# Two-layer encoder trunk on one Trainium2 core: block transposes share rooms, one input quarter changes from TensorE to blocks, four heads from blocks to TensorE

## Chip, cores and metric

The kernel runs on one core of one Trainium2 chip. The metric is the device time of one execution in microseconds; lower is better. All inputs are float32 in HBM, and so is the output, 256 tokens by 2048 features.

## What is computed

A trunk of two layers over 256 tokens, a grid of 4 x 64, with 2048 features. Each layer norms its input, projects it, runs 12 self-attention heads and 4 heads into 256 memory tokens, projects the 16 outputs back, adds them, and then runs a squared-ReLU MLP of width 8192.

```python
m = rms_norm(mem, mem_norm)
h = x
for i in range(2):
    n = rms_norm(h, attn_norm[i])
    if i == 0:    # neighbourhood attention with a relative-position bias
        q, k, v, qm = split(n @ a_w_in[0])
        mix = neighbourhood_attention(q, k, v, a_rpb[0])
    else:         # grouped queries: 12 query heads, 4 key heads
        q, k, v, qm = split(n @ b_w_in[0])
        q, k = axial_rope(rms_norm(q, b_q_norm[0])), axial_rope(rms_norm(k, b_k_norm[0]))
        mix = gqa_block_attention(q, k, v)
    km, vm = split(m @ w_mem_kv[i])
    cross = memory_attention(qm, km, vm)
    h = h + concat(mix, cross) @ w_o[i]
    n = rms_norm(h, mlp_norm[i])
    h = h + square(relu(n @ w_up[i])) @ w_down[i]
return rms_norm(h, final_norm)
```

## The kernel before

**Products.** Every float32 value is split into two parts, hi (a copy rounded to float32r, written by ScalarE, L441) and lo (value minus hi, written by VectorE, L442). A product is three TensorE instructions: hi with hi, hi with lo, lo with hi. Weights come from HBM in chunks of 1 MB (128 x 2048); SyncE's queue (SP) issues the loads, and each half of a chunk is split and then multiplied. Blocks of 512 output columns for two tiles of 128 tokens go through `m_products` (L314, 512-wide instructions), blocks with the tokens as the moving side through `products` (L334, 256-wide). A transpose is also a TensorE instruction (MATMUL with `ident`, 128 x 128).

**Order.** `plan` is the list of works in order. Each is cut into grains (a half chunk: 12 instructions of 512 columns). `run_all` goes through the grains: before each it traces the loads and splits of the grains ahead (3 grains for a plain work, 8/5/4 or 8/8/4 for those of the MLP), then the grain's products, then one tick. `later(n, fn)` queues a function for n ticks on. A scheduler orders each engine's instructions from this trace by priority and by its own timeline; after that the order on each engine is fixed. `past(fn, ins)` (L793) makes what fn issues come behind two given instructions, one on ScalarE and one on VectorE; `tc.issue_after(ins)` does so for the engine of one instruction; `pin` keeps program order.

**Memory.** Tiles with one tag of a pool share a number of rooms (`bufs`). A tile waits until the last user of its room is done. Pool `work` (right side) serves the attention stages; it is closed when an o projection starts and `side` is opened in its place until `to_work` (L1346) reverses that in the second layer. `ring` holds the weight chunks and their splits, `mlp` the MLP's. PSUM tags `acc` and `att` have four banks each.

**Two ways to transpose.** On TensorE: `transposed` (L453) and `attend2` (L516) put four 128 x 128 transposes per 256-wide pair into a PSUM bank, from which hi and lo are split. By blocks: VectorE transposes 32 x 32 blocks, and four transfers on SP's queue move the blocks between partition groups; `far_blocks` (L525) with `arrived` (L539) does that for a quarter (512 columns) of h, `turned` (L544) with `halved` (L559) for a head's probabilities. `far_blocks` needs a room for the blocks and a room for what lands.

**Attention.** `attention` (L578) spreads the steps of each head over ticks: scores and softmax (`attend`), the transpose, its split, and the product with the values (`attend3`). With four steps, (0, 1, 3, 4) or (0, 2, 5, 6), the transpose goes by blocks; with three, (0, 3, 6), by TensorE. In the second layer `b_qm_done` starts the four memory heads (one grain apart), and `b_q_done(blk)` starts heads 4 blk to 4 blk + 3; blocks 0 and 1 go by blocks, block 2 by TensorE. `normed_heads` (L1280) writes a block's normed and rotated heads into two tiles of tag `b_o` (three rooms), which `heads_T` transposes on TensorE.

**From the o projection to the up projection.** The o projection runs its four output blocks in two pairs (`add_o`). h is the residual; its root mean square is estimated from the first three blocks (`guard`, "near"), and the exact factor is applied later. When the third block (nb = 2) is added to h, `scaled(b)` for b = 0, 1, 2 at ticks 2, 3 and 5 scales a quarter of h (ScalarE, L819) into a tile of tag `T` and turns it by blocks into a tile of tag `b`, whose halves hold the blocks and what lands; `landed(b)` at ticks 4, 5 and 7 splits the four columns that arrived into `hT` (ScalarE L471, VectorE L472). Tags `T` and `b` have two rooms each. `begun` prepares the last quarter in a `T` tile; when the fourth block's products are done, VectorE adds them (L861), and TensorE transposes this quarter into bank `pt_n` (L459). The first up projection reads `hT` in order of k.

**From the MLP to the second layer.** The last eighth of the MLP (`plain_grains`) gives h its four blocks. `down_done(0, nb)` adds each (L1066), takes squares, and for nb < 3 turns the quarter by blocks (tick 1, two `T` tiles named `n_t`) and splits it into `nT` (tick 3); the last quarter goes through TensorE. The second layer begins with eight works for qm and k (L1352 on): quarters 0, 1 and 2 of qm, 0 of k, 3 of qm, then 1, 2 and 3 of k. The first three are loaded and split in pool `side`, the others in `ring`.

**The end.** `finish` (L1209) adds the last block of 512 columns in three pieces: all columns of tile 0, then the two 256-column halves of tile 1. For each, ScalarE squares and sums, VectorE adds the mean square to the running one, and behind a tile's last piece GpSimd takes the power -1/2, VectorE and ScalarE scale, and the rows are stored.

Of the kernel before, what the change touches and what calls it, by code (L numbers as in the profile page):

```python
# [70 lines left out]
class Work:  # L71


    def __init__(self, kind, src, acts, first, begins, last, start, done):
        self.kind, self.src, self.acts = kind, src, acts
        self.first, self.begins, self.last, self.start, self.done = first, begins, last, start, done
        self.early = self.behind = self.last_block = False
# [48 lines left out]
def encoder_kernel(ctx: ExitStack, tc: tile.TileContext, t: dict, out: bass.AP):  # L126
# [82 lines left out]
    box: dict = {}  # L209
# [5 lines left out]
    def halves_of(w):  # L215
# [9 lines left out]
        def prep(hf):  # L225
            if hf == 0:
                n = plan.index(w)
                if n in soon:
                    tiles["raw"] = soon.pop(n)
                else:  # L230
                    tiles["raw"] = at.ring.tile([P, CH], F32, tag="raw", bufs=3, name="raw")
                    nc.sync.dma_start(tiles["raw"], w.src)
            src = tiles["raw"][:, hf * HALF : (hf + 1) * HALF]
            if w.behind and hf == 1:

                tiles[hf] = new_half(w.kind)
                past(lambda: split(*tiles[hf], src), box["cat" if w.last_block else "pT", NH - 2])
            elif plan[plan.index(w) - 1].last_block:

                tiles[hf] = new_half(w.kind)  # L240
                past(lambda: split(*tiles[hf], src), box["cat", NH - 1])
            elif w.kind == "S" and hf == 0 and plan[plan.index(w) - 1].kind == "M":
                tiles[hf] = entered_half(src)
            else:
                tiles[hf] = new_half(w.kind)
                split(*tiles[hf], src)
# [269 lines left out]
    def attend2(sc):  # L516
        pt = at.att.tile([P, NT, SEQ], F32, tag="att", name="pt_a")
        for s in range(NT):
            i = NT - 1 - s
            for k in range(NT):  # L520
                nc.tensor.transpose(pt[:, k, i * P : (i + 1) * P], sc[:, s, k * P : (k + 1) * P], ident)
        pT = at.work.tile([P, 2, NT, SEQ], F32R, tag="pT", name="pT")
        return pT, split(pT[:, 0], pT[:, 1], pt)
# [15 lines left out]
    def arrived(dst, raw, k0, which):  # L539

        for n in range(4):
            split_pair(dst, raw[:, :, :, n], which, k0 + n, by_quarters=True)

    def turned(sc):  # L544
# [7 lines left out]
        pT = at.work.tile([P, 2, 4, NT, NT * 32], F32R, tag="pT", name="pT_t")  # L552
# [246 lines left out]
    def o_done(layer, nb):  # L799
# [16 lines left out]
        def scaled(b):  # L816
            y = at.side.tile([P, NT, 512], F32, tag="T", bufs=2, name="h_s")
            for i in range(NT):
                nc.scalar.activation(y[:, i, :], h[:, i, b * 512 : (b + 1) * 512], AF.Copy,  # L819
                                     scale=box["scale"][:, i : i + 1])  # L820
            room = at.side.tile([P, 2, 1024], F32, tag="b", bufs=2, name="h_t")
            box["raw", b] = far_blocks(lambda i: y[:, i, :], (room[:, 0], room[:, 1]))
# [13 lines left out]
        def f(w):  # L836
# [67 lines left out]
    def up_grains(layer, part, m):  # L904
# [24 lines left out]
        def run(hf):  # L929
# [14 lines left out]
            products(own["ps"], box["hT" if part else "hT0"], hf * (KT // 2), KT // 2, *own.pop(hf), keep_order=part > 0,  # L944
                     first=own.pop("first", None))
# [234 lines left out]
    def down_done(layer, nb):  # L1180
        def f(w):
# [27 lines left out]
    def finish(w, i, bank, begin, end):  # L1209
# [10 lines left out]
        q = small.tile([P, 1], F32, tag="ss0", name="ss_f")  # L1220
        sq = at.side.tile([P, 512], BF16, tag="junk", bufs=1, name="sq")
        nc.scalar.activation(sq[:, begin:end], hs, AF.Square, accum_out=q)
# [7 lines left out]
        m = box["mean"] = mean(q, box["mean"])  # L1230
# [49 lines left out]
    def normed_heads(w):  # L1280
        cg, sg = box["rope"]
        outs = []
        for i in range(NT):
# [10 lines left out]
            o = at.work.tile([P, 4, HD], F32, tag="b_o", bufs=3, name="b_o")  # L1294
# [22 lines left out]
    def b_q_done(blk):  # L1317
        def f(w):
# [5 lines left out]
                       for j, kv in enumerate(kvs)], 1, 2, (0, 3, 6) if blk == 2 else (0, 2, 5, 6),  # L1324
# [3 lines left out]
    def b_qm_done(w):  # L1328
# [3 lines left out]
        for i in range(NT):  # L1332
# [8 lines left out]
                   for j in range(NMH)], 1, 1)  # L1341
# [4 lines left out]
    def to_work():  # L1346
        closed("side")
        open_work()
        mem_back()
# [6 lines left out]
    plan[-6].early = "last"  # L1356
    add_m(blocks(4), parts_of("nT"), b_v_done)
# [13 lines left out]
    later(26, x_stats)  # L1371
# [132 lines left out]
```

## Time and profile before

| | us |
|---|---|
| median of three runs | 2013.01 |
| lowest, highest | 2012.42, 2015.40 |
| the profiled execution, its own time | 2015.48 |
| span of its instructions | 2013.7 |
| mean granted TensorE clock over the span | 0.998 |
| VectorE, ScalarE busy | 1703.7, 1270.0 |

A row of a timeline shows start, duration, engine, line, operation, output<-inputs, shape and count; in brackets the engine's idle time before it and what ended that. A row of a stretch shows its length and the busy time of TensorE, of its weight loads, of VectorE, ScalarE and GpSimd with instruction counts, then the granted clock, the share of the DMA engines and GB/s. TensorE's instructions overlap: one lasts longer than the distance to the next, so the rate is read from start to start (0.227 us for 512 columns, 0.113 to 0.12 for 256). A TensorE wait is idle time only where nothing else was in flight.

### The profile page before, as it was taken

To read this page: it belongs to the slowest core of one execution; us is meant where nothing else is said; L and a number is where in the kernel's file an instruction comes from. 1 tells how busy PE (TensorE), PEld (TensorE's weight loads), DVE (VectorE), ACT (ScalarE), POOL (GpSimd) and SP (SyncE) were. 2 spreads that over 40 slices of the span, in tenths; PEclk is the share of its full clock that TensorE was granted. 3 is DMA by queue.
4 is the path that set the end of the run, shared out by engine and by line. 5 is a ranking of instruction groups with operands and counts; after the bars stand their busy time and mean duration, and the time that the engine had idled before them with its cause. 6 is when DMAs were issued, how large, how long until landed. Compare 5 with 4: busy or idle time off the path is not lost.

```text
span 2013.7 us, 32879 instructions
## 1 busy us (share of the span) xinstructions
PE 1999.8 (99%) x12948; PEld 1815.4 (90%) x12948; DVE 1703.7 (85%) x2110; ACT 1270.0 (63%) x1732; POOL 117.7 (6%) x144
## 2 busy tenths in 40 slices
PE   9999999999999999999999999999999999999998
PEld 8999999899999999999988888789999999999997
DVE  6777777579999999999997769778999999999896
ACT  6655555466676666666655557566766666666664
POOL 0000000000000000000000001000000000000000
PEclk9999999999999999999999999999999999999999
DMA  8766655757777777777767455547777777777763
GB/s 294 303 196 209 211 193 195 262 164 248 229 230 234 231 222 235 232 233 234 229 205 261 157 206 181 208 147 236 234 231 232 232 234 235 228 239 223 236 215 131
DMA packets 103083, 445.93 MB, mean 221 GB/s; under 512 B 10896, under 2 KB 36496, under 8 KB 55440
## 3 DMA queue, kind: packets, MB, share of 16 engines
q1 hardware_dynamic: 85824, 411.84, 58.4%
q0 software_dynamic: 16816, 31.46, 9.0%
q8 instruction: 101, 1.65, 0.3%
q10 hardware_dynamic: 288, 0.52, 0.1%
q14 instruction: 54, 0.44, 0.1%
HBM read 398.17 MB, written 4.19 MB: 200 GB/s over the span
## 4 chain that ended last, share of the span: by engine, by line
PE 92%; DVE 3%; DMA 1%; ACT 1%; SPq 1%; issue 1%; DVEq 0%; POOL 0%; POOLq 0%; ACTq 0%
PE ps_u L346 34%; PE ps_s L346 10%; PE p L1025 9%; PE p L1026 9%; PE p L1023 9%; PE ps_m L326 7%; PE ps_m L323 7%; PE ps_m L327 7%; DMA pT_t<-sc_t 1%; DMA h_t<-h_t 1%; SPq L555 1%; DVE lo L442 1%; SPq L535 0%; ACT hi L441 0%; DVE h_t L532 0%
## 5 line engine op out<-in xcount | busy, mean ns | idle before, releaser
L346 PE MATMUL ps_u<-hT,uh 128*128 128x256 f32 x3780 | 659.1, 277 | 1.0 <-ACT hT L471 0.8
L346 PEld LDWEIGHTS ps_u<-hT,uh 128*128 128x128 f32 x3780 | 574.6, 188 | 6.7 <-ACT hT L471 1.1
L346 PE MATMUL ps_u<-hT,ul 128*128 128x256 f32 x1940 | 536.4, 277 | 0.0
L441 ACT ACTIVATE uh<-raw_U 128x1024 fp32r<-128x1024 f32 x266 | 282.1, 1061 | 248.7 <-PE ps_u L346 227.7
L346 PEld LDWEIGHTS ps_u<-hT,ul 128*128 128x128 f32 x1940 | 364.4, 188 | 0.0
L442 DVE TENSOR_TENSOR lo<-raw,hi 128x1024 fp32r<-128x1024 f32 (+1 forms) x215 | 255.0, 1190 | 114.3 <-ACT hi L441 113.7
L442 DVE TENSOR_TENSOR ul<-raw_U,uh 128x1024 fp32r<-128x1024 f32 x266 | 322.9, 1218 | 25.5 <-ACT uh L441 25.3
L441 ACT ACTIVATE hi<-raw 128x1024 fp32r<-128x1024 f32 (+1 forms) x215 | 222.7, 1039 | 176.1 <-PE ps_m L327 92.0
L441 ACT ACTIVATE bh<-b 128x2048 fp32r<-128x2048 f32 x112 | 215.3, 1922 | 98.3 <-PE p L1026 92.2
L442 DVE TENSOR_TENSOR bl<-b,bh 128x2048 fp32r<-128x2048 f32 x112 | 256.1, 2287 | 11.4 <-ACT bh L441 11.4
L442 DVE TENSOR_TENSOR tl<-t,th 128x1536 fp32r<-128x1536 f32 x112 | 196.5, 1754 | 42.2 <-ACT th L441 41.0
L441 ACT ACTIVATE th<-t 128x1536 fp32r<-128x1536 f32 x112 | 166.8, 1489 | 40.7 <-PE p L1026 38.7
L1026 PE MATMUL p<-bh,a_s 128*128 128x512 f32 x448 | 175.1, 391 | 0.0
L1025 PE MATMUL p<-bl,a_s 128*128 128x512 f32 x448 | 174.5, 390 | 0.2
L1023 PE MATMUL p<-bh,a_s 128*128 128x512 f32 x448 | 174.3, 389 | 0.0
L995 POOL DMA_DIRECT2D b<-b x112 | 97.0, 866 | 1133.2 <-DVE t L994 983.5
L346 PE MATMUL ps_s<-nT,hi 128*128 128x256 f32 x896 | 155.0, 276 | 0.0
L346 PEld LDWEIGHTS ps_s<-nT,hi 128*128 128x128 f32 x896 | 135.6, 188 | 0.2
L1023 PE MATMUL p<-th,a_s 128*128 128x512 f32 x336 | 131.4, 391 | 0.0
L1025 PE MATMUL p<-tl,a_s 128*128 128x512 f32 x336 | 131.2, 390 | 0.0
L1026 PE MATMUL p<-th,a_s 128*128 128x512 f32 x336 | 130.7, 389 | 0.0
L346 PE MATMUL ps_s<-nT,lo 128*128 128x256 f32 x448 | 124.0, 277 | 0.0
(273 smaller groups left out, 3581.9 us busy)
## 6 DMA issues: line engine op xcount, KB each, us to landing
raw_U<-in_w_up SPq DMA_DIRECT2D x128, 1024.0 KB, 4.9
b<-in_w_pair SPq DMA_DIRECT2D x112, 1024.0 KB, 4.9
raw<-in_w_o SPq DMA_DIRECT2D x32, 1024.0 KB, 4.9
b<-b POOLq DMA_DIRECT2D x112, 256.0 KB, 3.4
raw<-in_w_b SPq DMA_DIRECT2D x21, 1024.0 KB, 4.9
raw<-in_w_av SPq DMA_DIRECT2D x12, 1024.0 KB, 4.9
raw<-in_w_aq SPq DMA_DIRECT2D x12, 1024.0 KB, 5.1
raw<-in_w_ak SPq DMA_DIRECT2D x12, 1024.0 KB, 4.8
```

Source lines behind the costliest of these rows:

```text
L323: first = nc.tensor.matmul(ps, ah, hi[:, s], start=st, stop=False)
L326: nc.tensor.matmul(ps, ah, lo[:, s], start=False, stop=False)
L327: final = nc.tensor.matmul(ps, al, hi[:, s], start=False, stop=sp)
L346: ins = nc.tensor.matmul(ps, x, acts[:, k, part], start=k == n == 0, stop=k == KT - 1 and n == 2)
L441: first = nc.scalar.activation(dst_hi, src, AF.Copy)
L442: return first, nc.vector.tensor_tensor(dst_lo, src, dst_hi.bitcast(F32), op=ALU.subtract)
L555: nc.sync.dma_start(raw[:, a].rearrange("p k c -> p (k c)"), blocks[a * 32 : (a + 1) * 32].rearrange("p b k t j -> p (b k t j)"))
L995: nc.gpsimd.dma_start(b[:, 3, :], b[:, 1, :], accum_op=ALU.add)
L1023: ins = nc.tensor.matmul(ps, a[:, 0, ai, :], hi[:, s], start=begins, stop=False)
L1025: nc.tensor.matmul(ps, a[:, 0, ai, :], lo[:, s], start=False, stop=False)
L1026: nc.tensor.matmul(ps, a[:, 1, ai, :], hi[:, s], start=False, stop=ends)
```

## The change

The block transposes of the o projection's output share rooms: for b = 0 and 1 the scaled quarter lies in one half of the `b` tile, its blocks in the other, and what lands goes over the scaled quarter; b = 2 takes a `T` tile for these two and the blocks half of the first `b` tile. `scaled(2)` moves from tick 5 to 4, all of them come behind the newest weight split, and the first up product is held behind the last o product. The last quarter of the second layer's input is turned by blocks too, later ticks apply to quarters 2 and 3, and one weight split (of quarter 1 of k) comes behind the arrival. Block 1's heads (4 to 7) use the three-step way; `pT` has three rooms in the second layer, `b_o` two; the memory heads there start two grains apart. The mean squares at the start run one tick sooner, from other rooms. The last piece's mean square is one VectorE instruction.

```diff
+            elif w.waits and hf == 0:
+                tiles[hf] = new_half(w.kind)
+                past(lambda: split(*tiles[hf], src), box["arrived"])
...
-                split(*tiles[hf], src)
+                box["weights"] = split(*tiles[hf], src)
...
-        pT = at.work.tile([P, 2, NT, SEQ], F32R, tag="pT", name="pT")
+        pT = at.work.tile([P, 2, NT, SEQ], F32R, tag="pT", bufs=2 + box["layer"], name="pT")
...
-            split_pair(dst, raw[:, :, :, n], which, k0 + n, by_quarters=True)
+            box["arrived"] = split_pair(dst, raw[:, :, :, n], which, k0 + n, by_quarters=True)
...
-                sq = at.work.tile([P, 512], F32, tag="b_y2", name="sq")
+                sq = at.work.tile([P, 512], F32, tag="b_y", name="sq")
...
         def scaled(b):
-            y = at.side.tile([P, NT, 512], F32, tag="T", bufs=2, name="h_s")
+            if b < 2:
+                box["room", b] = at.side.tile([P, 2, 1024], F32, tag="b", bufs=2, name="h_t")
+                y = box["room", b][:, 0]
+            else:
+                y = at.side.tile([P, 1024], F32, tag="T", bufs=2, name="h_s")
...
-            room = at.side.tile([P, 2, 1024], F32, tag="b", bufs=2, name="h_t")
-            box["raw", b] = far_blocks(lambda i: y[:, i, :], (room[:, 0], room[:, 1]))
+            box["raw", b] = far_blocks(lambda i: y[:, i * 512 : (i + 1) * 512], (box["room", b % 2][:, 1], y))
...
-                for b in range(GUARD):
-                    later((2, 3, 5)[b], scaled, b)
-                    later((4, 5, 7)[b], landed, b)
-                later(7, begun)
+                for n, fn, *args in ((2, scaled, 0), (3, scaled, 1), (4, scaled, 2), (4, landed, 0), (5, landed, 1),
+                                     (7, landed, 2), (7, begun)):
+                    later(n, lambda fn=fn, args=args: past(lambda: fn(*args), box["weights"]))
...
+            with tc.issue_after(box["late"].ins) if part == m == hf == 0 else nullcontext():
+                products(own["ps"], box["hT" if part else "hT0"], hf * (KT // 2), KT // 2, *own.pop(hf),
+                         keep_order=part > 0, first=own.pop("first", None))
...
-            if nb < 3:
-                def turn():
-                    room = [at.side.tile([P, 1024], F32, tag="T", bufs=2, name="n_t") for _ in range(2)]
-                    box["raw"] = far_blocks(lambda i: h[:, i, nb * 512 : (nb + 1) * 512], room)
-                later(1, turn)
-                later(3, lambda: arrived(box["nT"], box["raw"], nb * 4, G_A1))
-            else:
-                later(1, transposed, box["nT"], lambda i, k: h[:, i, k * P : (k + 1) * P], list(range(12, KT)), G_A1)
+            def turn():
+                room = [at.side.tile([P, 1024], F32, tag="T", bufs=2, name="n_t") for _ in range(2)]
+                box["raw"] = far_blocks(lambda i: h[:, i, nb * 512 : (nb + 1) * 512], room)
+            def come():
+                arrived(box["nT"], box["raw"], nb * 4, G_A1)
+            for n, fn in (((1, turn), (3, come)), ((3, turn), (5, come)), ((1, turn), (4, come)))[max(nb - 1, 0)]:
+                later(n, lambda fn=fn: past(fn, box["splits"][-1]) if nb == 2 or nb == 3 and fn is turn else fn())
+            if nb == 3:
...
+        if begin:
+            m = small.tile([P, 1], F32, tag="rs_v", name="fin_v")
+            sq = at.side.tile([P, 3, 512], F32, tag="T", bufs=2, name="sq_t")[:, 0, : end - begin]
+            nc.vector.tensor_tensor_reduce(sq, hs, hs, 1.0 / D, box["mean"], ALU.mult, ALU.add, m)
+        else:
+            q = small.tile([P, 1], F32, tag="ss0", name="ss_f")
+            sq = at.side.tile([P, 512], BF16, tag="junk", bufs=1, name="sq")
+            nc.scalar.activation(sq[:, begin:end], hs, AF.Square, accum_out=q)
...
-            o = at.work.tile([P, 4, HD], F32, tag="b_o", bufs=3, name="b_o")
+            o = at.work.tile([P, 4, HD], F32, tag="b_o", bufs=2, name="b_o")
...
-                       for j, kv in enumerate(kvs)], 1, 2, (0, 3, 6) if blk == 2 else (0, 2, 5, 6),
+                       for j, kv in enumerate(kvs)], 1, 2, (0, 3, 6) if blk else (0, 2, 5, 6),
...
-                   for j in range(NMH)], 1, 1)
+                   for j in range(NMH)], 1, 2)
...
+        box["layer"] = 1
...
+    plan[-3].waits = True
...
-        later(3 + j, mem_squares, j)
+        later(min(3 + j, 9), mem_squares, j)
-    later(11, mem_stats)
+    later(10, mem_stats)
...
-    later(26, x_stats)
+    later(25, x_stats)
```

More of the change, by code (lines that the diff above doesn't have):

```diff
@@ L1 @@
 import math
-from contextlib import ExitStack
+from contextlib import ExitStack, nullcontext
 import numpy as np
@@ L76, in __init__ @@
         self.first, self.begins, self.last, self.start, self.done = first, begins, last, start, done
-        self.early = self.behind = self.last_block = False
+        self.early = self.behind = self.last_block = self.waits = False
 class Shifted:
@@ L206, in gain @@
         return gains[:, which * KT + k : which * KT + k + 1]
-    box: dict = {}
+    box: dict = {"layer": 0}
     plan: list = []
@@ L551, in turned @@
                                 sc[:, s, :].rearrange("p (k i b) -> p k b i", k=NT, b=4))
-        pT = at.work.tile([P, 2, 4, NT, NT * 32], F32R, tag="pT", name="pT_t")
+        pT = at.work.tile([P, 2, 4, NT, NT * 32], F32R, tag="pT", bufs=2 + box["layer"], name="pT_t")
         raw = pT[:, 1].bitcast(F32)
@@ L1229, in finish @@
             box["mean"] = v
-        m = box["mean"] = mean(q, box["mean"])
+            m = box["mean"] = mean(q, box["mean"])
         if end < 512:
```

7 lines of the change are left out of this document (1 added, 6 removed).

## The prediction

> **What bounds the kernel now.** I read the page first (its busy line), then the table of waits of TensorE, then TensorE's timeline around every wait in it, and last the other engines' timelines there.
>
> ```profile
> PE 1999.8 (99%) x12948; PEld 1815.4 (90%) x12948; DVE 1703.7 (85%) x2110; ACT 1270.0 (63%) x1732; POOL 117.7 (6%) x144
> ```
>
> TensorE (PE) sets the time: it is idle for 13.9 us of the 2013.7, and some 8 of those lie behind its last product. So a change can only give back what PE loses in stalls, add or remove PE instructions, or shorten the tail. The stalls:
>
> ```profile
> PE ps_m L323 <- ACT cat L441: 1.8, 2, 1.4
> PE av L570 <- DVE pT_t L442: 1.0, 1, 1.0
> ...
> PE ps_u L346 <- ACT hT L471: 0.8, 1, 0.8
> PE ps_m L326 <- DVE ul L442: 0.5, 1, 0.5
> PE pt_n L459 <- DVE h_s L861: 0.5, 2, 0.3
> ```
>
> Columns: total us, times, longest. They stand in four places: the second layer's last heads (cat, pT_t), the entry into each layer's up projection (hT, h_s), and the entry into the second layer (ul). A stall costs more than its idle time, as the granted clock shows:
>
> ```profile
> 1268.00:1272.00 4.00, 2.63 (x18) 2.24 (x17) 3.73 (x7) 3.93 (x11) 0.00 (x0) 1.00 0.42 172
> 1344.00:1348.00 4.00, 3.72 (x20) 3.52 (x19) 4.00 (x7) 3.75 (x6) 0.00 (x0) 0.63 0.00 0
> 1348.00:1352.00 4.00, 4.00 (x35) 4.00 (x34) 3.83 (x7) 2.13 (x6) 0.00 (x0) 0.94 0.76 266
> ```
>
> The column behind POOL is the clock: 0.63 and 0.94 behind the stall at 1342, that is 4 x 0.37 + 4 x 0.06 = 1.7 us of full speed lost, but 1.00 around the equally long stall at 1269.
>
> **The up projection's input, second layer.** The same instructions run at this place in both layers, so the layers can be laid side by side:
>
> ```profile
> 426.26 0.38 PE L459 MATMUL pt_n<-ident,h_s 128*128 128x128 f32 x2
> ...
> 427.54 0.40 PE L346 MATMUL ps_u<-hT,uh 128*128 128x256 f32 x2
> 428.11 0.87 PE L459 MATMUL pt_n<-ident,h_s 128*128 128x128 f32 x6 [0.17 <-DVE h_s L861]
> ...
> 431.44 0.28 PE L346 MATMUL ps_u<-hT,uh 128*128 128x256 f32 x1
> ...
> 1341.24 0.38 PE L459 MATMUL pt_n<-ident,h_s 128*128 128x128 f32 x2
> ...
> 1342.05 0.28 PE L346 MATMUL ps_u<-hT,ul 128*128 128x256 f32 x1
> 1343.18 0.91 PE L346 MATMUL ps_u<-hT,uh 128*128 128x256 f32 x2 [0.85 <-ACT hT L471]
> ...
> 1349.76 0.28 PE L346 MATMUL ps_u<-hT,uh 128*128 128x256 f32 x1
> ```
>
> From the pair of transposes to the last row layer 1 takes 431.44 - 426.26 = 5.18 us, layer 2 1349.76 - 1341.24 = 8.52: 3.34 us lost, the 1.7 of the clock among them. What is late is the third quarter of hT:
>
> ```profile
> 419.94 1.07 DVE L532 STREAM_TRANSPOSE h_t<-h_s 128x512 f32<-128x512 f32 x1
> 425.96 1.71 ACT L471 ACTIVATE hT<-h_t,first 128x256 fp32r<-128x256 f32 x4 [2.69 <-DMA h_t<-h_t]
> ...
> 1329.98 1.71 ACT L471 ACTIVATE hT<-h_t,first 128x256 fp32r<-128x256 f32 x4 [1.00 <-DMA h_t<-h_t]
> 1335.18 1.07 DVE L532 STREAM_TRANSPOSE h_t<-h_s 128x512 f32<-128x512 f32 x1
> 1342.62 1.71 ACT L471 ACTIVATE hT<-h_t,first 128x256 fp32r<-128x256 f32 x4 [4.10 <-DMA h_t<-h_t]
> ```
>
> Its blocks go into a room that the first quarter leaves only when its splits are done, behind 1329.98 + 1.71; the second transpose ends at 1336.25, and the split starts 6.4 us later (5.0 in layer 1). With shared rooms the blocks need only the first quarter's landing, 1329.98. Behind one weight split of 1.2 us and the two transposes of 1.07 they end near 1333, and the split starts 5.0 to 6.4 later, at 1338 to 1339.5. PE asks at 1342.2: 3 us of margin. So I take the whole **3.34** (1.6 without the clock's 1.7, should another wait bring it down there, to 3.34). The Trainium skill, "TensorE: Matmul & The Clock Gate", Part 1, lets the clock fall after a window of about 3.4 us without work; here it fell behind idle pieces of 0.85, 0.13 and 0.28 us, so the trace does not agree, and by the rule, with the drop owed to something else, the sum would come out 1.7 us higher.
>
> The 0.17 us wait of pt_n on h_s, in both layers, is VectorE finishing the third quarter before L861; starts 427.54 to 428.11 against 0.23 for two products make 0.34 us a layer; I take half of the two, **0.35** (0 to 0.7).
>
> The waits added here: scaled and landed come behind the newest weight split on ACT and DVE. That split is due in the same grain, and what queues behind it (squares of the mean, weight splits three grains ahead) has those grains' 2.7 us each as cover; price 0. The up weights' split into room "b" now waits for the third landing as well, about 1338, while PE first reads it at 1347: also 0. Holding the first up product behind the last o product only keeps the order that PE shows.
>
> **Heads 4 to 7 on TensorE.** In order: TensorE, then two ScalarE rows.
>
> ```profile
> 1259.13 1.04 PE L1276 MATMUL pt_h<-ident,b_o 128*128 128x128 f32 x8
> 1261.19 0.39 PE L570 MATMUL av<-pT_t,vb 128*128 128x256 f32 x1 [1.02 <-DVE pT_t L442]
> ...
> 1269.43 0.28 PE L497 MATMUL sc_ps<-kT,qT 128*128 128x256 f32 x1
> 1271.08 0.50 PE L323 MATMUL ps_m<-hi,cat 128*128 128x512 f32 x1 [1.37 <-ACT cat L441]
> 1271.42 0.40 PE L326 MATMUL ps_m<-lo,cat 128*128 128x512 f32 x1
> ...
> 1290.10 0.39 PE L570 MATMUL av<-pT,vb 128*128 128x256 f32 x1 [0.17 <-DVE pT L442]
> 1291.43 0.50 PE L323 MATMUL ps_m<-hi,cat 128*128 128x512 f32 x1 [0.47 <-ACT cat L441]
> ...
> 1253.01 0.48 ACT L508 ACTIVATE sc<-sc_ps,nm 128x256 f32<-128x256 f32 x1 [0.58 <-DVE sc_t L550]
> 1266.83 0.63 ACT L441 ACTIVATE pT_t<-pT_t 128x512 fp32r<-128x512 f32 x1 [2.86 <-DMA pT_t<-sc_t]
> ```
>
> Four stalls: idle 1.02 + 1.37 + 0.17 + 0.47 = 3.03 us. Each also costs 0.16 (a 256-wide product lasts 0.28 in a slot of 0.12) and 0.11 at the restart (1271.08 to 1271.42 is 0.34 against 0.23): 4 x 0.27 = 1.08, so 4.1 in all. Heads 6 and 7 are late because their probabilities go through blocks, four transfers and a split that waits for them, and because the blocks take one of three "sc" rooms, for which the exponential at 1253.01 waits. The new path has neither. I let the first two stalls go (2.93) and half of the last two (0.6), which are heads 8 to 11, already on this path: **-3.5** (0 to -4.1).
>
> The price is 16 transposes on PE. Eight took (1.04 - 0.27) / 7 = 0.11 us a start at 1259.13; the upper bound is this group:
>
> ```profile
> L521 PE MATMUL pt_a<-ident,sc 128*128 128x128 f32 x16 | 2.7, 272 | 0.0
> ```
>
> 2.7 / 16 = 0.17. So 1.8 to 2.7; I take **+2.1**, nearer the start-to-start figure, since a transpose between products overlaps them. VectorE loses eight block transposes (0.6 us each), SP 16 transfers; the split costs the same. The freed SP queue lets w_o loads go sooner; no wait of PE in the table is for one of them.
>
> A third pT room costs nothing; a third b_o room goes, which would matter if a block's heads were written before the last block's were transposed: those transposes are over at 1226, the next block writes from 1238, 12 us of cover. Memory heads two grains apart end at most three grains (8 us) later than 1164, and their first reader runs at 1226.
>
> **Input of the second layer, last quarter.** TensorE, ScalarE, SyncE:
>
> ```profile
> 1092.03 0.73 PE L323 MATMUL ps_m<-uh,nT 128*128 128x512 f32 x2
> 1093.30 0.50 PE L326 MATMUL ps_m<-ul,nT 128*128 128x512 f32 x1 [0.53 <-DVE ul L442]
> ...
> 1086.67 1.71 ACT L471 ACTIVATE nT<-n_t,first 128x256 fp32r<-128x256 f32 x4 [5.09 <-DMA n_t<-n_t]
> ...
> 1081.56 2.59 SPq L535 DMA_DIRECT2D n_t<-n_t  x4
> ...
> 1084.85 22.36 SPq L232 DMA_DIRECT2D raw<-in_w_b  x6
> ```
>
> ScalarE stood 5.09 us before the third quarter's split, so the weight split behind it came late and PE lost 1.27 - 0.45 = 0.82, with the restart 0.9. Moving that quarter two grains on, behind the weight split, takes the wait out of the way. Eight PE transposes go: 8 x 0.11 = 0.9. Together -1.8. Against that stand four more transfers on SP among the loads at 1084.85, and four products of VectorE and ScalarE each. The last quarter is first read by the fourth work of the q block, the fifth of the stage in program order: 24 products of 0.23 us a work from 1083.5 on make 1083.5 + 4 x 5.44 = 1105.3. VectorE can turn it from about 1094, when the third quarter's landing frees the rooms; with the 5.1 us from issue to split seen here it is split by about 1102. I take **-1.7** (from -1.8 to the second rival's loss).
>
> **Tail and start.**
>
> ```profile
> 2006.57 0.42 ACT L1222 ACTIVATE sq<-first 128x256 bf16<-128x256 f32 x1 [1.66 <-DVE first L1218]
> ...
> 2005.02 0.42 DVE L1232 TENSOR_TENSOR first<-first,gf 128x256 f32<-128x256 f32 x1
> ...
> 2007.11 0.16 DVE L1213 SCALAR_TENSOR_TENSOR fin_v<-ss_f,fin_v 128x1 f32<-128x1 f32 x1 [0.63 <-ACT sq L1222]
> ```
>
> From 2006.57 to 2007.27 the last mean square takes 0.70 on two engines; one VectorE instruction over 256 columns that also reads its sum takes between 0.42 (L1232) and 0.42 + 0.19 (ScalarE's sum read): **-0.2** (-0.3 to 0). The earlier mean squares at the start move no PE instruction out of a stall: 0 (+-0.2).
>
> **Sum**, against the profiled execution's 2015.48: -3.34 - 0.35 - 3.5 + 2.1 - 1.7 - 0.2 = -7.0, so 2008.5. The median of the runs shown, 2013.01, lies 2.5 below that execution; if its runs lack the 1.7 us at the low clock, the gain is 5.3 there, and 2013.01 - 5.3 = 2007.7. Between the two: **2008.0**.
>
> **Rivals.**
> - *Everything goes.* Last stalls of the heads and of h_s go too: another -0.95 and the low price of the transposes, -0.3: 2006.5 to 2007. For it: VectorE gets lighter at all four places.
> - *The second layer's last quarter is late (slower).* SP issues in order; if its four transfers stand behind the six loads, they are issued at 1107.2, landed and split by 1107.2 + 2.6 + 2.9 + 2 = 1114.7, and PE stands from 1105.3 for up to 9.4 us, and the low clock adds 1.7; the split that the change puts behind the arrival holds ScalarE and VectorE meanwhile. Time 2008.0 + 1.7 + 11.1 = 2020.8; it passes 2017.0 (0.2% slower) when the splits are done later than about 1111. Against it: of the stage's eight works six don't need that quarter, so PE can have work until 1116.
> - *The heads' stall moves.* ScalarE and VectorE feed heads 8 to 11 at the same pace, so half of the 4.1 us stays and the transposes are paid: +0.05 in place of -1.4: 2009.5 to 2010.5. For it: the two stalls at 1290 are on the new path already.
> - *Transposes let the clock fall.* If they did not count as work, eight of them with the 1.02 us idle behind would have cost the clock; one drop costs 1.7: 2009.7. The clock was 1.00 there (1268 to 1272 too). The Trainium skill, the same page, Part 4, says that transposes do not count as busy in the same way for the gate, and by that rule the 16 added would bring drops; the trace does not bear it out at 1259, where no drop follows.
>
> **Chances.** Forecast 0.50 (2006.8 to 2009.6), everything 0.18, moved stall 0.17, late quarter 0.09, clock 0.06. About 0.2% (4.0 us) is what a measurement of this kernel can tell from no change; that is 2009.0. Faster: 0.38 of the forecast's 0.50 and the 0.18, with 0.02 of the others: 0.58. Same: 0.12 + 0.15 + 0.05 + 0.03 = 0.35. Slower: 0.07 of the late quarter. Range 2005.5 to 2012.5, which leaves out most of the late quarter and the ends of the others.
>
> **What would show it.** Right: no wait of ps_u on hT near 1342 and a clock of 1.00 there; no waits on cat or pT_t near 1260 to 1271; 16 more pt_a and 8 fewer pt_n; no wait of ps_m on nT before 1110; the first power of the tail's last piece 0.2 us sooner behind the last product. Wrong: a wait on ACT nT in the second layer's entry, new waits on pT near 1250 to 1290, or products that start slower than 0.113 and 0.227 us apart with the rooms moved.

## The result, and the profile after

The changed kernel takes 2014.18 us (median of 14 runs, 2011.92 to 2015.31) beside 2013.16 for the kernel before on the same chip (14 runs): ratio 1.0002, 95% interval 0.9994 to 1.0011. No difference can be told. The forecast was 2008.0. The profiled execution of after took 2014.38 us, with a span of 2012.6.

Table of waits of TensorE, after (total us, times, longest); the first group that is new stands on top:

```profile
PE ps_m L327 <- ACT hi L445: 3.1, 1, 3.1
PE ps_m L327 <- ACT uh L445: 0.7, 1, 0.7
PE pt_n L463 <- DVE h_s L869: 0.6, 2, 0.3
```

The waits on cat, pT_t, hT and ul that the prediction quoted are gone; two waits for weight splits have come, at the entry into the second layer. TensorE's timeline there, after:

```profile
1093.83 0.39 PE L331 MATMUL ps_m<-uh,nT 128*128 128x512 f32 x1
1097.30 1.22 PE L327 MATMUL ps_m<-hi,nT 128*128 128x512 f32 x2 [3.09 <-ACT hi L445]
1099.20 1.22 PE L327 MATMUL ps_m<-uh,nT 128*128 128x512 f32 x2 [0.67 <-ACT uh L445]
1100.22 0.63 PE L330 MATMUL ps_m<-lo,nT 128*128 128x512 f32 x1
1100.64 0.63 PE L331 MATMUL ps_m<-hi,nT 128*128 128x512 f32 x1
```

and the stretches around it (granted clock in the column behind POOL):

```profile
1096.00:1100.00 4.00, 2.02 (x4) 1.21 (x5) 2.72 (x3) 3.81 (x4) 0.00 (x0) 0.59 1.06 407
1100.00:1104.00 4.00, 4.00 (x11) 3.10 (x11) 4.00 (x4) 2.05 (x3) 0.00 (x0) 0.55 1.11 311
1344.00:1348.00 4.00, 3.71 (x33) 3.52 (x32) 4.00 (x5) 2.15 (x4) 0.00 (x0) 1.00 0.00 0
```

TensorE stands 3.1 us, then 0.7, and then works at half clock: 1100.22 to 1100.64 is 0.42 us where 0.227 is the full rate. The clock is low from 1096.74 to 1103.57. At 1344, where it fell before, it is now 1.00.

To compare stages I use one measure below, TensorE's **loss**: over all neighbouring products of a stretch, the distance from start to start less 0.2266 us (512 columns), 0.1135 (256) or 0.11 (transposes), added up. Idle time, restarts and a low clock are all in it.

| loss, us | 0:160 | 1080:1120 | 1240:1320 | 1320:1400 |
|---|---|---|---|---|
| before | 5.4 | 0.9 | 4.9 | 5.3 |
| after | 5.4 | 6.9 | 1.0 | 1.0 |

The two later places gave back 8.2 us, more than forecast. The entry into the second layer took 6.0 of it, the 8 transposes more (16 added, 8 removed) 0.9; what is left, 1.4 (1.3 by these rounded losses), is by how much sooner the last product starts (2004.27 against 2005.67).

This profiled execution of before is a costly one at 1342. Of its 5.3 there, 1.7 are the low clock, and 1.4 come from 1348 to 1388, where the 256-wide products start 3.6% slower than 0.1135 us apart at a clock of 1.00. A second profile of the same kernel (experiment 11, called before again) has neither, and loses 2.2 there. The same stretch in before and in before again:

```profile
1368.00:1380.00 12.00, 12.00 (x104) 12.00 (x103) 9.21 (x14) 6.41 (x9) 0.94 (x1) 1.00 0.69 220
1368.00:1380.00 12.00, 12.00 (x109) 12.00 (x108) 8.65 (x11) 7.46 (x10) 1.02 (x2) 1.00 0.67 212
```

Against before again the change gives back 5.2 us at the two later places and 0.7 at the start, and loses 6.1 at the entry and 0.9 for transposes; its last product starts 0.9 later (2004.27 against 2003.38), which is near what the medians show.

**What is late at 1094.** ScalarE's timeline, then SyncE's queue, then GpSimd, all after:

```profile
1088.81 1.06 ACT L445 ACTIVATE uh<-raw_U 128x1024 fp32r<-128x1024 f32 x1 [1.15 <-PE ps_m L331]
1092.21 1.72 ACT L475 ACTIVATE nT<-n_t,first 128x256 fp32r<-128x256 f32 x4 [2.34 <-DMA n_t<-n_t]
1096.19 2.00 ACT L445 ACTIVATE hi<-raw 128x1024 fp32r<-128x1024 f32 x2 [2.26 <-DMA raw<-in_w_b]
1098.10 1.99 ACT L445 ACTIVATE uh<-raw_U 128x1024 fp32r<-128x1024 f32 x2
...
1083.04 1.93 SPq L539 DMA_DIRECT2D n_t<-n_t  x3
1085.01 0.60 SPq L909 DMA_DIRECT2D raw_U<-in_w_b  x1
1085.66 0.61 SPq L539 DMA_DIRECT2D n_t<-n_t  x1
1086.31 2.21 SPq L232 DMA_DIRECT2D raw<-in_w_b  x3
...
1088.15 0.71 POOL L1218 TENSOR_TENSOR rstd<-full,mhalf 128x2 f32<-128x2 f32 x1 [69.23 <-DVE full L794]
1088.82 0.60 POOL L677 DMA_DIRECT2D km<-mem_k  x1
```

ScalarE, then GpSimd, before:

```profile
1090.94 1.04 ACT L441 ACTIVATE uh<-raw_U 128x1024 fp32r<-128x1024 f32 x1
1092.26 2.01 ACT L441 ACTIVATE hi<-raw 128x1024 fp32r<-128x1024 f32 x2 [0.28 <-DMA raw<-in_w_b]
1094.18 1.04 ACT L441 ACTIVATE uh<-raw_U 128x1024 fp32r<-128x1024 f32 x1
...
1091.51 0.71 POOL L1205 TENSOR_TENSOR rstd<-full,mhalf 128x2 f32<-128x2 f32 x1 [72.71 <-DMA raw<-in_w_b]
1092.34 0.60 POOL L673 DMA_DIRECT2D km<-mem_k  x1
```

Call the stage's works 1, 2, 3 and so on. A work is 24 products, two halves of 12, and each split named uh is one half. From 1085.89 to 1094.05 TensorE runs 36 products of uh with nT: work 1 and the first half of work 2 (split at 1088.81). What it lacks then is weights: the second half of work 2 is the first of the two splits from 1098.10. On ScalarE this split stands behind that of the first ring chunk (the two splits of raw from 1096.19). The order was the same before (1090.94, 1092.26, 1094.18), but there the chunk had landed at 1092.24. The third quarter of nT is not what TensorE waits for: it is split from 1092.2 to 1095.9, and its first reader, work 3, starts only near 1109.

Three things changed together. TensorE comes sooner: without the wait and the transposes that stood there it is through the first half of work 2 at 1094.05, before at 1095.7. The chunk is issued 1.5 us later (1086.31 against 1084.85), since the transfers of the third quarter stand ahead of it on SyncE's queue and begin 1.5 us later (1083.04 against 1081.56). And it takes 9.9 us (1086.31 to 1096.17) where before it took 7.4. The longer transfer has a neighbour that was not there before: the reload of the memory keys and values, which GpSimd issues behind the power of rstd. The mean square for rstd no longer queues behind the third quarter's split, so the power comes 3.4 us sooner and the reload 3.5. Which of these costs what had to be tried.

### The profile page after: what moved, and what is told of

Read it like the earlier page. It is cut to its first block, busy times and chain, and to the rows that moved or that the text cites. A ratio compares the mean times of both kernels' runs of the same rounds, so it can differ in the third digit from the quotient of the medians.

```text
span 2012.6 us, 32835 instructions
## 1 busy us (share of the span) xinstructions
PE 1997.9 (99%) x12956; PEld 1812.4 (90%) x12956; DVE 1703.2 (85%) x2105; ACT 1270.2 (63%) x1730; POOL 117.8 (6%) x144
## 4 chain that ended last, share of the span: by engine, by line
PE 93%; DMA 2%; DVE 2%; ACT 1%; issue 1%; SPq 0%; POOL 0%; POOLq 0%; DVEq 0%; ACTq 0%
PE ps_u L350 33%; PE p L1035 9%; PE p L1036 9%; PE p L1033 9%; PE ps_s L350 8%; PE ps_m L330 7%; PE ps_m L331 7%; PE ps_m L327 7%; DMA raw<-in_w_b 0%; ACT hi L445 0%; DMA raw_l<-in_w_km 0%; PE sc_ps L500 0%; PE av L573 0%; PE av L574 0%; PE sc_ps L499 0%
```

## The experiments

**1. Third quarter back on its old ticks**, the last one still by blocks.

```diff
-for n, fn in (((1, turn), (3, come)), ((3, turn), (5, come)), ((1, turn), (4, come)))[max(nb - 1, 0)]:
-    later(n, lambda fn=fn: past(fn, box["splits"][-1]) if nb == 2 or nb == 3 and fn is turn else fn())
+for n, fn in ((1, turn), (4, come)) if nb == 3 else ((1, turn), (3, come)):
+    later(n, lambda fn=fn: past(fn, box["splits"][-1]) if nb == 3 and fn is turn else fn())
```

> The changed kernel, but the third quarter of the second layer's input keeps its old ticks (turned one grain on, split three grains on, not behind a weight split); the last quarter still goes by blocks. Measure: how much TensorE loses between 1080 and 1120 us against one product every 0.227 us (0.9 us before the change, 6.9 after). Theory A, the third quarter was moved too far: with it split some 6 us sooner PE has the third work of the q block to do again while the first ring chunk comes; loss 1 to 2 us, time about 2014.2 - 5 = 2009. Theory B, the first ring chunk is late because other transfers run beside it: it still lands after 1094, loss 3 to 5 us, time 2010.5 to 2012.5. Theory C, the last quarter's own blocks are to blame: loss stays near 6.9, time 2014.

Measured 2011.21 us, before 2013.22; ratio 0.9988 (0.9979 to 0.9997). Loss 1080:1120 is 4.2. The reload moves with the third quarter (issued at 1091.8 again) and the chunk lands at 1091.6. The 4.2 lies in theory B's range, but the chunk is not late any more, so no theory had it in this shape. ScalarE, then TensorE:

```profile
1104.67 1.71 ACT L475 ACTIVATE nT<-n_t,first 128x256 fp32r<-128x256 f32 x4 [7.21 <-DMA n_t<-n_t]
...
1091.63 0.73 PE L327 MATMUL ps_m<-uh,nT 128*128 128x512 f32 x2 [0.97 <-ACT uh L445]
1092.89 0.50 PE L330 MATMUL ps_m<-ul,nT 128*128 128x512 f32 x1 [0.53 <-DVE ul L446]
...
1107.38 0.73 PE L327 MATMUL ps_m<-hi,nT 128*128 128x512 f32 x2 [0.53 <-ACT hi L445]
1108.64 0.50 PE L330 MATMUL ps_m<-lo,nT 128*128 128x512 f32 x1 [0.53 <-DVE lo L446]
```

Some 2.6 us go between 1088 and 1100, where the transposes of the last quarter had stood, and 1.6 at 1104 to 1109, where ScalarE stands 7.2 us for the last quarter and the weight split ordered behind it is late. So the move of the third quarter (theory A) cost a part, the fall from 6.9 to 4.2, but not in A's way: here too work 3 comes behind the chunk, and what came sooner is the chunk. Another part, 1.6, is the weight split ordered behind the last quarter, which is nearest to theory C, though the loss did not stay near 6.9.

**2. Reload held back**: one GpSimd instruction that reads two columns of the second ring chunk stands in front of it (`mem_back` is traced two ticks later, so that this chunk is known).

```diff
+g = nc.gpsimd.tensor_tensor(gate[:, :NT], box["ring2"][:, :NT], mhalf[:, :NT], op=ALU.mult)
+with tc.issue_after(g.ins):
     nc.gpsimd.dma_start(box["km"], mem_k)
...
```

> The changed kernel, but the reload of the memory keys and values on GpSimd's queue (issued from 1088.8 in the changed kernel, from 1092.3 before) waits until the second ring chunk has landed: one GpSimd instruction that reads two columns of that chunk stands in front of it. The order of all other engines is the same. Theory A (third quarter too late): the third quarter is split as late as before, near 1095.9, but the ring chunk decides what PE starts with; if the chunk lands where it did (1096.2) the loss stays 6 to 7 us, time 2014. Theory B (the reload shares the DMA engines with the ring chunk): the chunk lands about 1.9 us sooner, near 1094.3; the wait of 3.1 us falls to about 1.2, and with it perhaps the stretch at half clock (3.4 us more): loss 1.5 to 5 us, time 2009 to 2012.3. Theory C (last quarter): no change, 2014.

2011.47 us; ratio 0.9991 (0.9982 to 1.0). Loss 4.5. ScalarE and TensorE:

```profile
1093.83 2.01 ACT L447 ACTIVATE hi<-raw 128x1024 fp32r<-128x1024 f32 x2 [0.73 <-DMA raw<-in_w_b]
...
1094.94 0.73 PE L329 MATMUL ps_m<-hi,nT 128*128 128x512 f32 x2 [1.26 <-ACT hi L447]
1096.83 1.22 PE L329 MATMUL ps_m<-uh,nT 128*128 128x512 f32 x2 [1.16 <-ACT uh L447]
```

The chunk now takes 8.3 us (issued at 1085.56) against 9.9, so the reload beside it cost 1.6; in experiment 4, where the reload went out only at 1106, the chunk took 7.9. The wait falls from 3.1 to 1.3 and the half clock from 6.8 us to 3.4. Theory B holds, for 2.4 of the 6.0 (these 2.4 and the parts found with experiments 1 and 8 overlap and do not add up).

**3. The whole second layer's input as before**, all else changed (the loop of `down_done` as in the old code, and no `waits`).

> The changed kernel with the whole second layer's input as it was: third quarter on its old ticks, last quarter through TensorE (8 transposes more), no weight split behind the arrival. All other parts of the change stay. If this part alone ate the gain (A, B or C): loss between 1080 and 1120 back to about 0.9, time 2014.2 - 6.0 + 0.9 for the transposes = 2009 (2008 to 2009.5). If the loss there comes from elsewhere (the other parts push the stage): loss 4 to 7, time 2013 to 2015.

2008.41 us (2007.72 to 2010.41); ratio 0.9977 (0.9968 to 0.9986). Loss 0.8. This part of the change ate the gain of the others. TensorE here:

```profile
1089.95 0.38 PE L463 MATMUL pt_n<-ident,first 128*128 128x128 f32 x2
...
1090.63 0.82 PE L463 MATMUL pt_n<-ident,first 128*128 128x128 f32 x6
1091.21 0.72 PE L327 MATMUL ps_m<-uh,nT 128*128 128x512 f32 x2
1092.46 0.50 PE L330 MATMUL ps_m<-ul,nT 128*128 128x512 f32 x1 [0.53 <-DVE ul L446]
```

The eight transposes run while TensorE would have to wait for the weight split at 1091 anyway. In experiment 1, with the third quarter on the same ticks but without these transposes, the same place has waits of 0.97 and 0.53: removing the transposes saved nothing.

**4. Only the new input, on the kernel before.**

> The kernel before with only the new treatment of the second layer's input (later ticks for the third quarter, last quarter by blocks, one weight split behind the arrival). A, B or C: it loses the 6 us alone and saves the 8 transposes' 0.9: 2013.2 + 5.0 = 2018 (2017 to 2019.5). If the loss needs the other parts too: 2012.5 to 2014.

2014.86 us; ratio 1.0008 (0.9999 to 1.0016): less harm than expected, and by the time alone not told from none. Loss 1080:1120 is 2.75, with waits of 1.0 and 1.2 at the same two splits as in experiment 2, but the clock stayed at 1.00 and the reload, held by another room, went out only at 1106. So the loss at the entry does not need the other parts, but with them it is larger. This execution also lost some 1.6 us between 428 and 472, where the products ran 3.6% slow (see the end). And the loss at 1342 had vanished (loss 1320:1400 of 0.6), although that code was the old one. That put the largest term of the prediction in doubt.

**5, 6, 7. One of the other parts alone, on the kernel before**: the rooms; the heads; the mean squares at start and end. Each edit is the lines of the diff that belong to it.

> The kernel before with only the shared rooms of the block transposes between the o and the up projection (with the new ticks and the order behind the weight splits). Theory P (the prediction): the second layer's entry lost 3.34 us in every execution and the rooms give it back: 2013.2 - 3.3 - 0.35 = 2009.5 (2009 to 2010.5). Theory J: the loss at 1342 was an event of the one profiled execution, in which one of four transfers landed 4.2 us after its issue instead of 2.7; a typical execution has at most the idle waits of pt_n there, so the rooms move the median by 0 to -0.8: 2012.4 to 2013.2.

> The kernel before with only the heads' part of the change (heads 4 to 7 on TensorE, three rooms for pT, two for b_o, memory heads two grains apart). The prediction's sum: -3.5 + 2.1 = -1.4, 2011.8. With the price that the other runs' counts suggest (16 x 0.11 = 1.76) and all four stalls gone (TensorE's loss between 1240 and 1320 us from 4.9 to about 1.0): -3.9 + 1.8 = -2.1, 2011.1. Rival (the stall moves to heads 8 to 11): loss 2.5 to 3 stays there, 2012.6 to 2013.2. Beside it, the second layer's entry of the kernel before is seen once more: Theory P says a loss near 3.3 us between 1320 and 1360, Theory J about 0.5.

> The kernel before with only the mean squares: at the start one tick sooner and from other rooms, at the end one VectorE instruction for the last piece. The prediction's sum: 0 and -0.2, 2013.0. The rival from the other traces: TensorE's loss in the first 160 us falls from 5.4 to 4.4 with the start's part, so -1.0 - 0.3 = 2011.9. And the second layer's entry of the kernel before once more: P a loss near 3.3 between 1320 and 1360, J about 0.5.

| | us | ratio, interval | 0:160 | 1240:1320 | 1320:1400 |
|---|---|---|---|---|---|
| rooms | 2011.79 | 0.9990 (0.9981, 0.9999) | 5.6 | 5.0 | 0.9 |
| heads | 2010.17 | 0.9983 (0.9974, 0.9992) | 6.0 | 0.9 | 0.9 |
| mean squares | 2011.71 | 0.9991 (0.9982, 1.0000) | 4.6 | 4.9 | 3.8 |

(before 2013.59 us, 33 runs.) The rooms bring 1.8 by the medians, between theories P and J. The heads bring 3.4, more than the 2.3 of their own stage (loss -4.1, 16 transposes at 0.11 +1.8), since the loss at 1342 is gone there too. The mean squares bring 1.9, where the prediction had 0.2. Each interval is some 1.8 us wide to either side, so only the heads' gain is well clear of none. The three sum to 7.1, and all together (experiment 3) bring 4.8; the loss at 1342, which the rooms and the heads each remove, counts twice in the 7.1. The loss at 1342 is seen in the run with the mean squares and not in the one with the heads, with the same code: something else decides. (The 3.8 has no drop of the clock in it, but the same slow stretch as before's profile, 1.6 us from 1344 to 1388.)

**8. Experiment 1 without the order behind the arrival.**

```diff
-    plan[-3].waits = True
```

> The changed kernel with the third quarter on its old ticks (as in the earlier run that had only this) and without the order that puts the first weight split of quarter 1 of k behind the arrival of the last quarter. In that earlier run TensorE lost 4.2 us between 1080 and 1120: 2.6 at 1088 to 1100 where the eight transposes had stood, 1.6 at 1104 to 1109 behind that weight split. If the order behind the arrival costs the second part, it goes: loss 2.6, time 2011.2 - 1.6 = 2009.6. If the last quarter itself is late by then, PE waits for nT instead and the loss stays 3.5 to 4.5: 2011. The first part should stay, since nothing covers the wait for the weight split any more.

2008.82 us (2008.15 to 2009.47); ratio 0.9973 (0.9964 to 0.9982). Loss 2.5: the 1.6 at 1104 to 1109 is gone, nT of the last quarter is not late, and the waits of 1.0 and 0.5 stay where the transposes had been. So the last quarter by blocks can be had, and gains nothing: 0.9 for the transposes, and 1.7 more of loss than in experiment 3; beside before, both are 4.8 us faster.

The 6.0 come apart in three steps: from after to experiment 1 the third quarter's later ticks, 6.9 to 4.2; from there to experiment 8 the split ordered behind the arrival, 4.2 to 2.5; from there to experiment 3 the wait that the transposes had covered, 2.5 to 0.8.

**9, 10, 11. What makes hT late at 1342?** The DMA queues between 1340.0 and 1341.2, before (packets, MB, share of the 16 engines):

```profile
q1 hardware_dynamic: 223, 0.11, 40.7%
q8 instruction: 1, 0.02, 4.9%
```

One packet of 16 KB that loads instructions takes 0.95 us (4.9% of 16 engines over 1.2 us, one engine's time) while the four transfers of h_t run. The last of the four landed 4.2 us after its issue; the three others and all eight of the quarters ahead took 2.7 to 3.1. There are 101 such loads to 12,948 products, one for 128 on average, so a change in the number of TensorE's instructions moves all those behind it. Three runs: before with 2 instead of 10 idle products at the start; the heads' part with 2; before again.

```diff
-    for _ in range(10):
+    for _ in range(2):
         nc.tensor.matmul(idle, ones, ones, start=True, stop=True)
```

> The kernel before with 2 instead of 10 idle products of TensorE at its very start, nothing else: 8 float32 products fewer, so every load of 16 KB of instructions falls later in TensorE's stream (all those behind the start). Theory F: the third quarter's last transfer landed late at 1342 because one load of instructions (at 1340.2, 0.95 us on one DMA engine, 3.9 us behind the first of the four issues) ran among them; in the runs where the count of TensorE's instructions before this place was 16 lower or 32 higher it fell elsewhere and no wait on hT was left. Then here it falls 1.4 to 1.8 us later, behind the transfers: the four transfers land 2.7 to 3.0 us after their issues, no wait on hT, loss between 1320 and 1400 about 0.6 to 0.9 in place of 5.3. Rival, the loss belongs to the rooms and the late issue alone: wait on hT of 0.8 to 1.0 stays, loss 3.8 to 5.3. The start can lose up to 1.5 us, since the clock rises later; median 2012 to 2013.5 by F, 2013.5 to 2015 by the rival.

> The run with only the heads' part (16 transposes more), again with 2 instead of 10 idle products at the start: the 16 transposes moved the load of instructions to 1.7 us behind the first of the four issues, and the fewer idle products bring it back by about as much, to 3 to 3.9 us behind it. Theory F: the wait on hT comes back, the last transfer lands 3.9 to 4.5 us after its issue, loss between 1320 and 1400 from 0.9 to 3.5 to 5; median about 2010.2 + 2 to 3. Rival (lighter engines at this place had taken the wait away): no wait on hT, loss 0.9, median 2010.2 to 2011.

> The kernel before once more, for a second profile of it. Theory F: the load of instructions falls at the same place among the transfers, 3.5 to 4 us behind the first issue, one of the four lands about 4.2 us after its issue, and TensorE waits 0.8 to 1.0 us for hT; loss between 1320 and 1400 of 3.8 (clock kept) or 5.3 (clock fallen). If it was an event of that one execution: no wait on hT, loss 0.6 to 0.9.

ScalarE's split of the third quarter, first in before again, then in before with 2 idle products, then in the heads' part with 2:

```profile
1343.35 1.71 ACT L471 ACTIVATE hT<-h_t,first 128x256 fp32r<-128x256 f32 x4 [4.08 <-DMA h_t<-h_t]
```

```profile
1342.85 1.71 ACT L471 ACTIVATE hT<-h_t,first 128x256 fp32r<-128x256 f32 x4 [2.71 <-DMA h_t<-h_t]
```

```profile
1340.93 1.71 ACT L471 ACTIVATE hT<-h_t,first 128x256 fp32r<-128x256 f32 x4 [2.73 <-DMA h_t<-h_t]
```

| | load of instructions behind first issue, us | issue to landing of the four, us | wait on hT | loss 1320:1400 |
|---|---|---|---|---|
| before | 3.9 | 2.8, 2.8, 3.0, **4.2** | 0.8 | 5.3 |
| before again | 3.9 | 2.8, 2.8, 3.0, **4.2** | 0.8 | 2.2 |
| only mean squares | 3.7 | 2.8, 2.8, **4.5, 4.3** | 1.0 | 3.8 |
| only heads | 1.7 | **4.0, 3.7, 3.5, 3.2** | none | 0.9 |
| only input | 5.2 | 2.8, 2.8, 2.7, 2.8 | none | 0.6 |
| before, 2 idle | 7.2 | 2.8, 2.8, 2.7, 2.8 | none | 1.2 |
| heads, 2 idle | 5.4 | 2.7, 2.8, 2.7, 2.8 | none | 0.6 |

Run 9 bears out theory F: with nothing changed but the start, the load falls behind the transfers, all four land in time and no wait on hT is left. Its time is 2013.71 us (ratio 1.0000, 0.9991 to 1.0009), because the start loses 8.2 instead of 5.4 us. In before again it lost 6.1. Run 11 shows the load and the wait again, so the wait is not one execution's accident; its loss of 2.2 lies below the 3.8 that I expected with the clock kept, because the slow stretch behind it is missing too. The clock fell in only one of the three executions that waited. Run 10 missed: the 8 idle products are 16 entries in the trace, and the load moved by 3.7 us, past the transfers and not onto them. No wait came back (2010.86 us), which both theories allow with the load there, so it doesn't tell them apart. In the run with only the heads the load delays all four transfers, but the last still lands 5.2 us behind the first issue; in before it was 6.2.

The thirteen traces hold more such cases. They have 312 block transfers of the o projection's output, of both layers. The 296 with no load running in the 2.8 us behind their issue landed 2.7 to 3.1 us after it; the 16 with one took 3.0 to 4.5. That the load makes the transfer late does not rest on run 9 alone.

## Why the prediction was wrong

**The second layer's last quarter (-1.7): this step failed.** Against experiment 3 the new input costs 6.0 us of loss less 0.9 for the transposes, so +5.1 in place of -1.7; by the medians 2014.18 - 2008.41 = 5.8. The step said that "Moving that quarter two grains on, behind the weight split, takes the wait out of the way". It takes that wait out, but the next weight split, of work 2's second half, stands on ScalarE behind that of the first ring chunk, and the move makes this chunk late: issued 1.5 us later and 2.5 longer on its way, it lands 3.9 us later, while TensorE comes 1.7 us sooner. TensorE stands 3.1 us and then loses the clock. I asked for the due time of the last quarter alone, not for that of the next weights. Nor did I cost what the mean square's power lets loose on GpSimd's queue: the reload of 2 MB beside the chunk (2.4 us of the 6.0, experiment 2). The split ordered behind the last quarter's arrival, which the sum leaves out, is 1.7 (experiment 1 against 8). The 0.9 for the transposes was no gain, because they covered a wait for a weight split (experiments 1, 3 and 8). The rival on a late quarter did not come in its own form: the last quarter landed by 1107.0 and was split later than the 1102 I gave it, but no product waited for it in after, nor for the third quarter, which the sign "a wait on ACT nT" named. Open is how much the later issue of the chunk costs by itself: experiment 1 undoes it together with the early reload, and no run moves it alone.

**The up projection's input (-3.34): right that it goes, wrong about its cause and its usual size.** In the traces the loss 1320:1400 falls from 5.3 to 1.0 (the clock's part with it), but from 2.2 in before again: the 1.7 of the clock, which I took whole, is not there in every execution. And the rooms were only one half of the cause: the prediction noted 6.4 us from transpose to split against 5.0 in layer 1 and did not ask for the 1.4. They are the load of instructions (experiments 9 and 11): without it the four landed in 2.8 in place of 4.2. So an edit that shifts TensorE's instruction count could take the stall away too, and the heads' part and the input's part did, each alone. By the medians the rooms alone gave 1.8. The late room made the transfers so late that 1.4 us mattered. With the shared rooms they go sooner: in after ScalarE splits this quarter at 1339.7 instead of 1342.6, and TensorE does not wait.

**h_s (-0.35):** nothing; both waits remain, 0.6 us in all. **Heads (-3.5 + 2.1):** all four stalls went, loss -3.9 to -4.1, and the transposes cost 16 x 0.11 = 1.8, the lower end of the bounds. The step was right, and 0.8 us too cautious. **Start (0):** missed; experiment 7 loses 0.5 less between 40 and 80 and 0.4 less between 80 and 120, and the executions with this part lose 4.6 to 5.4 in the first 160 us against 5.4 to 6.1 in those without (the two with 2 idle products left out). With the tail's 0.3 that is 1.2 of the 1.9 by which experiment 7 is faster. **Tail (-0.2):** the sum's instruction is there:

```profile
2005.11 0.48 DVE L1237 CUSTOM_DVE_ANT_0 sq_t<-first,fin_v 128x256 f32<-128x256 f32 x1
2005.52 0.08 DVE L1237 DVE_READ_ACCUMULATOR2_ANT fin_v<- 128x1 f32 x1
2005.68 0.55 POOL L1254 TENSOR_TENSOR fin_r<-fin_v,mhalf 128x1 f32<-128x1 f32 x1 [4.43 <-DVE fin_v L1237]
```

The last power starts 1.41 us behind the last product's start (2004.27), before it was 1.68: -0.27 as forecast. But the time from that product's end to the end of the span is 8.05 against 7.73, and over the executions here it lies between 7.7 and 8.0 with the old tail and between 7.5 and 8.1 with the new one, so the gain can't be seen in the whole.

**The transposes and the clock.** In after the clock has no drop between 1103.57 and 2008, so none at the heads on TensorE; that rival is out.

**The sum.** The version of experiment 3 is the change without the failed step. Its 2008.41 lies near the 2008.0 that I had for the whole, by luck in part, since errors cancel: the start and the heads gave more than forecast, the rooms less, and the -1.7 never came. Its interval (0.9968 to 0.9986) lies clear below the kernel before, as does that of experiment 8 at 2008.82.

## What to carry to other kernels

Before a late input is moved out of a queue's way, write down what TensorE runs next, when it runs out of it, and what stands ahead of the next weights on each engine and each queue; a wait of an engine that is not the bottleneck may be the cheap side of the trade. When an instruction is released earlier, look at what stands behind it on its queue, since a transfer that starts sooner can land on another that is urgent. And TensorE work that can be removed is only a gain if TensorE has something else to do at that place. One profile can hold a costly execution: look at a second one before its loss is put into a sum.

## What the hardware showed

- A load of 16 KB of instructions took 0.9 to 2.0 us (median 0.97, 101 in each of the thirteen traces), and a transfer of 128 KB with such a load in its first 2.8 us landed 0.2 to 1.7 us later (3.0 to 4.5 against 2.8). The Trainium skill, "Runtime: NRT & Kernel Launch", section "Instruction fetch mechanics", has these blocks of 256 instructions and calls their cost mostly hidden; one for 128 products, each with its weight load, agrees with the block, and the engine itself did not wait: in before it has no idle piece between the load at 1340.2 and the wait on hT at 1342.3. The cost came out in another transfer.
- A drop of the clock between products lasted 3.41 us in before and in experiment 2, and 6.83 in after, twice that. It came within a wait of 3.1 us (after), after 1.26 and 1.16 us within 3.5 us (experiment 2), and in one of three executions after a wait of 0.8 to 1.0 with pieces of 0.1 and 0.3 behind it; it did not come after 1.01 and 1.16 us in experiment 4. The Trainium skill, "TensorE: Matmul & The Clock Gate", Part 1, has a window of about 3.4 us; the length agrees, and waits far below the window were enough.
- In three of the thirteen traces the 256-wide products behind an entry into an up projection ran 3.6% slow for some 40 us (loss of 0.15 us in every 4) at a clock of 1.00: before from 1348 and experiment 7 from 1344 in the second layer, experiment 4 from 428 in the first. What does that stays open.
